# Background steps held behind a weight load, and gate products spread over two kinds of PSUM banks, in a two-layer decoder trunk

## The chip, the core and the metric

The kernel runs on one core of a Trainium2 chip. A core has TensorE for matmuls (PE in the profile, with its weight loads as PEld), VectorE (DVE), ScalarE (ACT), GpSimd (POOL) and SyncE (SP), which here issues nearly all DMAs. The metric is the time of one execution on the device in microseconds (us), the median of several runs; lower is better.

## What is computed

A trunk of two layers over one sequence of 1024 tokens with 1024 features, all in float32. Layer 0 mixes tokens by attention, layer 1 by a state-space scan with a gated output. Each mixer is followed by a channel mixer with 4096 hidden features. All four are wrapped in a modulation (scale, shift, gate) that comes from one vector c, and in a layer norm:

```
for i in range(2):
    shift, scale, gate = modulation(silu(c), mod_mix_w[i], mod_mix_b[i])
    h = x * (1 + scale) + shift
    y = mla_mixer(h, ...) if i == 0 else s5_mixer(h, ...)
    x = layer_norm(ALPHA * x + (1 + gate) * y, ...)
    shift, scale, gate = modulation(silu(c), mod_ffn_w[i], mod_ffn_b[i])
    h = x * (1 + scale) + shift
    a = relu(h @ w1[i] + b1[i]);  y = (a * a) @ w2[i] + b2[i]
    x = layer_norm(ALPHA * x + (1 + gate) * y, ...)

# the end of s5_mixer
g = gelu(y)
z = g * sigmoid(g @ w_glu + b_glu)
return z @ w_out
```

## The kernel before

**Products in three passes.** Every large product splits both float32 operands into a high part (rounded for TensorE's fast float32 format) and a low part, the rest, and sums three matmuls: high by high, high by low, low by high. `split` makes the two parts, the high one on ScalarE (L74) and the low one on VectorE or GpSimd (L75); `mm3` issues the three matmuls (L78, L79, L80). So one block of 128 hidden features against 512 tokens is 8 x 3 = 24 matmuls of 128 x 128 by 512.

**Stages in time.** Attention runs to about 444 us, with its output product; the first channel mixer from there to 1222; the state-space mixer to about 1440; its gate products to 1532; its output product to 1645; the second channel mixer to the end. The parameters of the state-space mixer and the modulations of layer 1 do not depend on x. They are computed in the background of the first channel mixer.

**PSUM in these stages.** There are eight banks of 128 x 512 float32: two for transposes (tag `tr`), two for first products (`psA`, tag `a1`, in the profile `a`, taken by `a1_tile`) and four for the wide products (`psM`, tag `mm`, taken by `mm_half`, or two at a time by `mm_tile`).

**The channel mixer** (`mlp`, a generator that its caller drives step by step). The hidden features come in NJ = 32 blocks. `load1(j)` loads a block of w1 (512 KB on SP, L997) and splits it; `load2(j)` loads a block of w2 (L1004), multiplies it by the gate row (L1005) and splits it. Both loads use the same two raw buffers (tag `wr`). `mm1(j, h)` computes one block of hidden features for one half of the tokens into an `a1` bank: 24 matmuls, relu and square on ScalarE (L1026, L1027), the high part (L1028) and the low part on VectorE (L1029), which frees the bank. `mm2(js, h)` multiplies two blocks by w2 for four tiles of 128 tokens, each into two `mm` banks, and `accumulate` adds them to the rows X on VectorE (L829).

The head of the mixer loads three blocks of w1, runs five first products while the last rows still come from attention, loads two blocks of w2, and has GpSimd turn all eight row tiles into the residual (`residual`, L885 and L886). The last rows are normed on VectorE (L849 to L860) and ScalarE, transposed on TensorE (L874), scaled on ScalarE (L877) and split (L880, L881) into `hT`. Then a loop over g from 0 to 13 does per round two loads of each kind, four first products (three in the round g = 0, since its first was done in the head) and the wide products of the two blocks before.

**The background.** `bg` chains 48 steps of the two modulations, one flush and 75 steps of `s5_params`. A step of a modulation (`mod_block`) loads two pieces of a modulation weight, 256 KB each, on SP (L561) into small raw buffers, and folds each into an accumulator: the first of eight on GpSimd (L563), the others on VectorE (L568). `hv` holds these buffers: two accumulators and two raw ones (named `mb` in the profile), and from the product of block 5 on four raw ones more (`mr`). At the end of eight pieces TensorE sums the accumulator over partitions by small matmuls (L582, L588). `mlp` calls `tick(w)` after each first product with w = 2 and after each tile of a wide product with w = 1; a credit grows by w times `pace`, and each whole credit runs one step of `bg`. What is left at the first tile of the last wide product is run at once (`finish0`).

**The gate products.** For each of eight blocks m of w_glu, the block is loaded (L1466) and split, then each half of the tokens gets a product of 24 matmuls into an `a1` bank, a sigmoid (L1475), a multiplication by g (L1476) and a split into `zT`. The output product (`o_tiles`) follows; its first call works on three tiles of tokens at once, two in four `mm` banks and the third in the two `a1` banks.

**What sets the order.** The Python program traces all instructions; a planner at compile time then orders each engine's instructions along a simulated timeline, the earlier traced first where several are ready, and a tile waits until a buffer of its tag is free. Each engine and each DMA queue then runs its list strictly in that order. `tc.issue_after(ins)` adds an order without a wait: what the block traces on the engine of `ins` is listed behind `ins`.

Of the kernel before, what the change touches and what calls it, by code (L numbers as in the profile page):

```python
# [39 lines left out]
def kernel(  # L40
# [13 lines left out]
    V, S, P, PE, SY = nc.vector, nc.scalar, nc.gpsimd, nc.tensor, nc.sync  # L54
# [18 lines left out]
    def split(hi, lo, src, eng=None):  # L73
        S.activation(hi, src, AF.Copy)  # L74
        (eng or V).tensor_tensor(lo, src, f32(hi), ALU.subtract)  # L75
# [221 lines left out]
    ps = tr4()  # L297
# [161 lines left out]
    for t in range(8):  # L459
        zn[t] = f0.tile([128, 512], F32, tag="zn", name="zn", bufs=8)  # L460
        if t == 7:
            for v, vt in ((v1, vt1), (v2, vt2)):
                ps = tr4()
# [58 lines left out]
    gffn = cst.tile([128, 1024], F32, name="gffn")  # L522
# [90 lines left out]
    def step(gen, n=1, late=0):  # L613
        if late:
            with tc.high_priority(offset=-late):
                step(gen, n)
            return
        for _ in range(n):
            next(gen, None)
# [3 lines left out]
    bg = chain(mod_block(mod_mix_w[0], mod_mix_b[0], None, 2, "row", grow, pj, hv, on_pool=True),  # L623
               mod_all(0, mod_ffn_w[0], mod_ffn_b[0], 48, 0, 0, gffn, pj, hv, on_pool=True), mod_flush(hv))
# [194 lines left out]
    def mm_half():  # L819
        return psM.tile([128, 512], F32, tag="mm", name="mm")  # L820
# [13 lines left out]
    def a1_tile():  # L834
        return psA.tile([128, 512], F32, tag="a1", name="a1")
# [85 lines left out]
    wp = pool("wp", bufs=2)  # L921
# [6 lines left out]
    rb = res_row(wp, ln_mix_b[0], gb2=(gffn, mlp_b2[0]))  # L928
# [24 lines left out]
    hT = [[pa2.tile([128, 8, 512], F32R, tag="pa", name="hT") for _ in range(2)], None]  # L953
# [24 lines left out]
    def mlp(l, hT, bufs_, gate, wp, bg, finish, w1x, rb, pace=0.0):  # L978
        w1b, w2b, ab = bufs_
        w1r = mlp_w1[l].rearrange("(k p) (j f) -> j p k f", p=128, f=128)  # L980
        last = NJ - 1

        def w1_buf(j):
            return w1x if j == 0 else w1b[j % 2]

        def w2_buf(j):
            return w2b[j % 3] if j < last else tuple(q.rearrange("p k f -> p (k f)") for q in w1b[1])

        def a2_buf(j, h):
            return ab[3 * h + j % 3] if j < last else w1b[0][h].rearrange("p k f -> p (k f)").rearrange(  # L990
                "p (s f) -> p s f", s=2)

        def load1(j):
            if j >= NJ:
                return
            r = wp.tile([128, 8, 128], F32, tag="wr", name="w1r")
            SY.dma_start(r, w1r[j])  # L997
            split(*w1_buf(j), r)

        def load2(j):  # L1000
            if j >= NJ:
                return
            r = wp.tile([128, 1024], F32, tag="wr", name="w2r")
            d = SY.dma_start(r, mlp_w2[l][j * 128:(j + 1) * 128, :])  # L1004
            V.tensor_tensor(r, r, gate, ALU.mult)  # L1005
            split(*w2_buf(j), r)
            return d.ins

        credit = [0.0]

        def tick(w):
            credit[0] += w * pace
            while credit[0] >= 1.0:
                step(bg)
                credit[0] -= 1.0

        def mm1(j, h):
            wh, wl = w1_buf(j)
            hh, hl = hT[h]
            ps = a1_tile()  # L1020
            for k in range(8):
                mm3(ps, wh[:, k], wl[:, k], hh[:, k], hl[:, k], k == 0, k == 7)
            if l == 0 and j == 5 and h == 0:
                hv.r += Halves([wp.tile([128, 1024], F32, tag="r4", name="mr", bufs=2) for _ in range(2)]).all
            a2 = a2_buf(j, h)
            S.activation(ps, ps, AF.Relu, bias=vt2[:, l * 32 + j:l * 32 + j + 1])  # L1026
            S.activation(ps, ps, AF.Square)  # L1027
            S.activation(a2[:, 0], ps, AF.Copy)  # L1028
            V.tensor_tensor(a2[:, 1], ps, f32(a2[:, 0]), ALU.subtract)  # L1029
            tick(2.0)  # L1030

        def mm2(js, h):
            for t in range(4 * h, 4 * h + 4):
                ps = mm_tile()
                sl = slice((t % 4) * 128, (t % 4) * 128 + 128)
                for hf in range(2):
                    cs_ = slice(hf * 512, hf * 512 + 512)
                    for j in js:
                        a2, (wh, wl) = a2_buf(j, h), w2_buf(j)
                        mm3(ps[hf], a2[:, 0, sl], a2[:, 1, sl], wh[:, cs_], wl[:, cs_], j == js[0], j == js[-1])  # L1040
                if js[-1] == last:
                    finish(t, ps)
                else:
                    accumulate(t, ps)
                    tick(1.0)

        for j in range(3):
            load1(j)
        split_ = yield
        for j in range(3):  # L1050
            mm1(j, 0)
            split_ = (yield) or split_
        mm1(0, 1)
        mm1(1, 1)
        with tc.issue_after(split_):
            load2(0)
            d = load2(1)
        with tc.issue_after(d):
            ra = res_row(wp, ln_mix_g[l], name="ra")
        for t in range(8):  # L1060
            residual(t, ra, rb)
        for g in range(NJ // 2 - 2):
            j = 2 * g + 2
            load1(j + 1)
            if g:
                mm1(j, 0)
            mm1(j, 1)
            load2(j)
            mm2((j - 2, j - 1), 0)
            load1(j + 2)  # L1070
            mm1(j + 1, 0)
            mm2((j - 2, j - 1), 1)
            mm1(j + 1, 1)
            load2(j + 1)
        load1(last)
        mm1(last - 1, 0)
        mm1(last - 1, 1)
        load2(last - 1)
        mm1(last, 0)
        mm1(last, 1)  # L1080
        load2(last)
        js = tuple(range(NJ - 4, NJ))
        mm2(js, 0)
        mm2(js, 1)
# [8 lines left out]
    for t in range(2, 8):  # L1093
        ps = o_tiles([nxt], WO.__getitem__, t == 7)[0]
# [264 lines left out]
        if t == 5:  # L1359
            u_load(0)  # L1360

    mixer = mlp(0, hT, cont, gffn, wp, bg, finish0, w1x, rb, pace=0.6)
    next(mixer)
    mixer.send(o_end(7, ps))
    step(mixer, 100)
# [98 lines left out]
    for m in range(8):  # L1464
        r = wp.tile([128, 8, 128], F32, tag="wr", name="wgr")
        SY.dma_start(r, wgr[m])  # L1466
        gh, gl = [wp.tile([128, 8, 128], F32R, tag=g, name="wg", bufs=n)
                  for g, n in ((("r4", 2), ("r4", 2)) if m % 2 == 0 else (("k4", 1), ("a4", 1)))]
        split(gh, gl, r)
        for hf in range(2):  # L1470
            sl = slice(hf * 512, hf * 512 + 512)
            ps = a1_tile()
            for k in range(8):
                mm3(ps, gh[:, k], gl[:, k], gTh[k][:, sl], gTl[k][:, sl], k == 0, k == 7)
            S.activation(ps, ps, AF.Sigmoid, bias=vt1[:, VGLU + m:VGLU + m + 1])  # L1475
            V.tensor_tensor(ps, gTf[m][:, sl], ps, ALU.mult)  # L1476
            split(zT[hf][0][:, m], zT[hf][1][:, m], ps)
# [95 lines left out]
```

## Time and profile before

| | us |
|---|---|
| timed runs, median of 3 | 2366.98 |
| lowest and highest of them | 2361.97, 2376.51 |
| the profiled execution | 2353.56 |
| its span, first to last instruction | 2351.4 |
| VectorE busy in the span | 1420.1 (60%) |
| ScalarE busy | 831.6 (35%) |
| GpSimd busy | 626.5 (27%) |

The mean granted clock of TensorE over the span is 0.978 of full speed. A row of the windows gives a stretch, its length, the busy time and number of instructions of PE, PEld, DVE, ACT and POOL, the granted clock, and the busy share and rate of the DMA engines. A row of the timeline gives start, duration, engine, line, operation and operands, and in brackets how long the engine had been idle and what ended that. A row of the waits gives who waited for whom: total us, times, longest. Matmuls overlap in the pipeline, so their durations add up to more than the time they take.

### The profile page before, as it was taken

To read this page: it belongs to the slowest core of one execution; us is meant where nothing else is said; L and a number is where in the kernel's file an instruction comes from. 1 tells how busy PE (TensorE), PEld (TensorE's weight loads), DVE (VectorE), ACT (ScalarE), POOL (GpSimd) and SP (SyncE) were. 2 spreads that over 40 slices of the span, in tenths; PEclk is the share of its full clock that TensorE was granted. 3 is DMA by queue.
4 is the path that set the end of the run, shared out by engine and by line. 5 is a ranking of instruction groups with operands and counts; after the bars stand their busy time and mean duration, and the time that the engine had idled before them with its cause. 6 is when DMAs were issued, how large, how long until landed. Compare 5 with 4: busy or idle time off the path is not lost.

```text
span 2351.4 us, 29181 instructions
## 1 busy us (share of the span) xinstructions
PE 2241.3 (95%) x11039; PEld 1885.4 (80%) x11039; DVE 1420.1 (60%) x2473; ACT 831.6 (35%) x1399; POOL 626.5 (27%) x731
## 2 busy tenths in 40 slices
PE   7799998979999999999998998999999999999996
PEld 6678886867788788888888997878788888888885
DVE  8877786387777766676444445454744444444437
ACT  3477774442222323333235233324322222222321
POOL 5534767371000334333021212433500000000005
PEclk8899998989999999999999999999999999999998
DMA  7222224135453345446123554330211111111201
GB/s 257 62 62 61 85 99 170 32 111 167 150 163 113 96 110 144 127 116 158 51 81 144 162 167 157 108 99 28 72 54 45 45 59 40 54 54 36 63 27 72
DMA packets 191579, 229.44 MB, mean 98 GB/s; under 512 B 45361, under 2 KB 136764, under 8 KB 189390
## 3 DMA queue, kind: packets, MB, share of 16 engines
q1 hardware_dynamic: 186558, 214.98, 29.4%
q0 software_dynamic: 3840, 12.59, 1.7%
q8 instruction: 87, 1.43, 0.2%
q14 instruction: 54, 0.44, 0.1%
q10 hardware_dynamic: 1040, 0.00, 0.0%
HBM read 190.88 MB, written 34.54 MB: 96 GB/s over the span
## 4 chain that ended last, share of the span: by engine, by line
PE 48%; DVE 3%; DMA 2%; ACT 1%; issue 1%; SPq 0%; POOL 0%; DVEq 0%; ACTq 0%; POOLq 0%
PE a L78 8%; PE a L80 8%; PE a L79 8%; PE mm L78 7%; PE mm L79 7%; PE mm L80 7%; PE mm L1392 1%; DMA wor<-in_ssm_w_out_dram 1%; DMA pt<-prm_d 1%; DVE ct L75 1%; PE a L1419 0%; PE a L1418 0%; PE a L1417 0%; DVE wo L75 0%; DVE X L1518 0%
## 5 line engine op out<-in xcount | busy, mean ns | idle before, releaser
L829 DVE TENSOR_TENSOR X<-X,mm 128x512 f32<-128x512 f32 x478 | 322.6, 684 | 286.1 <-PE mm L80 282.2
L78 PE MATMUL mm<-pb 128*128 128x512 f32 x512 | 203.0, 397 | 5.8 <-DVE X L829 5.8
L78 PE MATMUL a<-hT,pb 128*128 128x512 f32 x496 | 195.6, 394 | 11.0 <-DVE pb L1029 10.7
L79 PE MATMUL mm<-pb 128*128 128x512 f32 x512 | 199.7, 390 | 0.0
L80 PE MATMUL mm<-pb 128*128 128x512 f32 x512 | 199.7, 390 | 0.0
L80 PE MATMUL mm<-ct 128*128 128x512 f32 x512 | 199.2, 389 | 0.0
L79 PE MATMUL mm<-ct 128*128 128x512 f32 x512 | 199.2, 389 | 0.0
L78 PE MATMUL mm<-ct 128*128 128x512 f32 x512 | 198.5, 390 | 0.0
L78 PE MATMUL a<-hT,ct 128*128 128x512 f32 x496 | 193.3, 390 | 3.3 <-DVE ct L1029 3.3
L1026 ACT ACTIVATE a<-a,vt 128x512 f32<-128x512 f32 x128 | 83.5, 652 | 314.5 <-PE a L80 314.3
L80 PE MATMUL a<-hT,pb 128*128 128x512 f32 x496 | 194.4, 392 | 0.0
L79 PE MATMUL a<-hT,pb 128*128 128x512 f32 x496 | 194.4, 392 | 0.0
L80 PE MATMUL a<-hT,ct 128*128 128x512 f32 x496 | 193.1, 389 | 0.0
L79 PE MATMUL a<-hT,ct 128*128 128x512 f32 x496 | 193.0, 389 | 0.0
L885 POOL TENSOR_TENSOR X<-X,rb 128x1024 f32<-128x1024 f32 x6 | 14.8, 2480 | 634.5 <-ACT X L861 634.5
L1005 DVE TENSOR_TENSOR w2r<-w2r,gffn 128x1024 f32<-128x1024 f32 x64 | 87.6, 1371 | 132.4 <-DMA w2r<-in_mlp_w_dram 132.3
L78 PEld LDWEIGHTS a<-hT,pb 128*128 128x128 f32 x496 | 94.0, 190 | 31.7 <-DVE pb L1029 12.4
L78 PEld LDWEIGHTS mm<-pb 128*128 128x128 f32 x512 | 96.2, 188 | 27.3 <-DVE X L829 7.5
L78 PEld LDWEIGHTS mm<-ct 128*128 128x128 f32 x512 | 95.9, 188 | 20.9 <-DVE X L829 0.6
L80 PEld LDWEIGHTS mm<-pb 128*128 128x128 f32 x512 | 96.1, 188 | 20.2
L79 PEld LDWEIGHTS mm<-ct 128*128 128x128 f32 x512 | 96.2, 188 | 20.0
L79 PEld LDWEIGHTS mm<-pb 128*128 128x128 f32 x512 | 96.2, 188 | 19.7 <-issue 0.7
(492 smaller groups left out, 5414.5 us busy)
## 6 DMA issues: line engine op xcount, KB each, us to landing
w1r<-in_mlp_w_dram SPq DMA_DIRECT2D x64, 512.0 KB, 4.1
w2r<-in_mlp_w_dram SPq DMA_DIRECT2D x64, 512.0 KB, 3.3
pt<-prm_d SPq DMA_DIRECT2D x16, 1536.0 KB, 7.2
mb<-in_mod_mix_w_dram SPq DMA_DIRECT2D x41, 256.0 KB, 2.6
prm_d<-cb SPq DMA_DIRECT2D x80, 128.0 KB, 2.4
wm<-in_mod_mix_w_dram SPq DMA_DIRECT2D x8, 1024.0 KB, 11.8
mb<-in_mod_ffn_w_dram POOLq DMA_DIRECT2D x32, 256.0 KB, 3.0
mb<-in_mod_ffn_w_dram SPq DMA_DIRECT2D x32, 256.0 KB, 3.0
```

What stands on the lines that cost most here:

```text
L75: (eng or V).tensor_tensor(lo, src, f32(hi), ALU.subtract)
L78: PE.matmul(ps, lh, rh, start=start, stop=False)
L79: PE.matmul(ps, lh, rl, start=False, stop=False)
L80: PE.matmul(ps, ll, rh, start=False, stop=stop)
L829: V.tensor_tensor(xh, xh, ps[h], ALU.add)
L885: P.tensor_tensor(X[t], X[t], ra, ALU.mult)
L1005: V.tensor_tensor(r, r, gate, ALU.mult)
L1026: S.activation(ps, ps, AF.Relu, bias=vt2[:, l * 32 + j:l * 32 + j + 1])
L1392: PE.matmul(pvv[i][:, g * 128:g * 128 + 128], pt[:, i, g], ug[:, g], start=True, stop=True)
```

## The change

In `mlp`, `load1` now returns the DMA of the block it loads. `tick` does nothing, and counts no credit, until the list `behind` has an entry. In the loop each round with g > 0 appends the DMA of its `load1(j + 1)`; the first is that of block 5, the sixth load of w1, in the round g = 1. From then on each background step is traced inside `issue_after` of that DMA, so that the DMAs it issues on SP stand behind it in SP's list. The pace goes from 0.6 to 0.66 for the first channel mixer; the second has an empty background. In the gate products the second half of the tokens takes its bank from the four `mm` banks instead of the two `a1` banks.

```diff
@@ load1 @@
-            SY.dma_start(r, w1r[j])
+            d = SY.dma_start(r, w1r[j])
             split(*w1_buf(j), r)
+            return d.ins
@@ tick @@
         credit = [0.0]
+        behind = []
 
         def tick(w):
+            if not behind:
+                return
             credit[0] += w * pace
             while credit[0] >= 1.0:
-                step(bg)
+                with tc.issue_after(behind[0]):
+                    step(bg)
                 credit[0] -= 1.0
@@ the loop of mlp @@
             j = 2 * g + 2
-            load1(j + 1)
+            d = load1(j + 1)
             if g:
+                behind.append(d)
                 mm1(j, 0)
@@ the first channel mixer @@
-    mixer = mlp(0, hT, cont, gffn, wp, bg, finish0, w1x, rb, pace=0.6)
+    mixer = mlp(0, hT, cont, gffn, wp, bg, finish0, w1x, rb, pace=0.66)
@@ the gate products @@
-            ps = a1_tile()
+            ps = a1_tile() if hf == 0 else mm_half()
```

## The prediction

> **What bounds the kernel now.** I read the page's first part, then the windows by stage, then TensorE's waits stage by stage, and at last the timelines of the two places where TensorE waits.
>
> ```profile
> PE 2241.3 (95%) x11039; PEld 1885.4 (80%) x11039; DVE 1420.1 (60%) x2473; ACT 831.6 (35%) x1399; POOL 626.5 (27%) x731
> ```
> ```profile
> 480.00:560.00 80.00, 63.83 (x268) 51.78 (x267) 67.70 (x69) 25.45 (x42) 50.91 (x20) 0.87 0.41 133
> 560.00:600.00 40.00, 38.15 (x172) 31.32 (x171) 26.91 (x38) 11.18 (x16) 0.69 (x1) 1.00 0.52 159
> 600.00:1222.00 622.00, 619.72 (x2841) 512.15 (x2840) 410.18 (x752) 181.40 (x293) 141.29 (x153) 1.00 0.42 118
> 1440.00:1532.00 92.00, 88.40 (x392) 72.46 (x391) 37.80 (x42) 31.34 (x44) 38.82 (x31) 1.00 0.30 98
> ```
>
> The columns are the stretch, its length, the busy time of PE, PEld, DVE, ACT and POOL, the granted clock and the DMA share. TensorE sets the time: it is busy 95% of the span, and in the long loop of the first channel mixer (600 to 1222 us) it is idle for 2.3 us in 622. What can be won lies where it is idle. Two such places are touched: the head of the first mixer, idle 80 - 63.83 + 40 - 38.15 = 18.0 us, and the gate products, idle 3.6 us. Who ends these waits, in the head and then in the gate products:
>
> ```profile
> PE a L78 <- DVE pb L1029: 10.7, 1, 10.7
> PE mm L78 <- DVE X L829: 4.9, 3, 1.9
> PE tr L588 <- DVE mb L568: 2.2, 1, 2.2
> ```
> ```profile
> PE a L78 <- DVE zT L75: 3.4, 1, 3.4
> ```
>
> In the head every wait is for VectorE, which is busy 67.7 of the 80 us. What fills it (VectorE's groups, 476 to 536 us):
>
> ```profile
> L568 DVE SCALAR_TENSOR_TENSOR mb<-mb,csT 128x512 f32<-128x512 f32 x12 | 24.5, 2041 | 1.3 <-DMA mb<-in_mod_mix_w_dram 0.7 <-POOL mb L563 0.5
> ```
>
> L568 is a background step. Twelve of them take 24.5 us of 60, at 2041 ns each. In the loop, with GpSimd's residual rows done, the same operation is short:
>
> ```profile
> L568 DVE SCALAR_TENSOR_TENSOR mb<-mb,csT 128x512 f32<-128x512 f32 x17 | 12.8, 750 | 0.5
> ```
>
> After two of the waits the clock drops:
>
> ```profile
> 495.00:500.00 5.00, 4.91 (x14) 3.68 (x15) 3.58 (x8) 3.66 (x8) 5.00 (x3) 0.50 0.19 56
> 500.00:505.00 5.00, 5.00 (x20) 4.04 (x19) 5.00 (x2) 1.06 (x1) 5.00 (x3) 0.84 0.00 0
> 525.00:530.00 5.00, 3.33 (x8) 2.66 (x9) 5.00 (x4) 0.00 (x0) 5.00 (x2) 0.50 0.53 160
> 530.00:535.00 5.00, 5.00 (x19) 3.98 (x18) 5.00 (x4) 0.14 (x1) 4.36 (x2) 0.77 0.59 207
> ```
>
> Busy time times the missing part of the clock gives 4.91 x 0.50 + 5.00 x 0.16 = 3.3 us and 3.33 x 0.50 + 5.00 x 0.23 = 2.8 us lost. So the head can yield at most 10.7 + 4.9 + 2.2 + 3.3 + 2.8 = 23.9 us, and the gate products 3.4 us.
>
> **The change part by part.** Before, a tick comes 24 units ahead of group g = 1 (five first products of 2, then the group g = 0 with three more products and eight tiles), which makes 24 x 0.6 = 14 background steps. The mixer has 240 units. After, the first 24 do nothing and the other 216 run at 0.66: 142 steps in place of 144. The background has 124 (48 for the two modulations, 1 flush, 75 for the state-space parameters), so it ends at unit 24 + 124/0.66 = 212 in place of 207, still 28 units, nearly two groups, ahead of the end. Nothing is removed; 14 steps go from the head into the 13 groups behind, with 28 loads on SP, 24 or 25 operations of L568 (the first of every eight is GpSimd's) and their small matmuls.
>
> **Term 1, the long wait.** VectorE before the product that TensorE waits for:
>
> ```profile
> 511.02 2.87 DVE L568 SCALAR_TENSOR_TENSOR mb<-mb,csT 128x512 f32<-128x512 f32 x1 [0.52 <-POOL mb L563]
> ...
> 517.17 2.81 DVE L568 SCALAR_TENSOR_TENSOR mb<-mb,csT 128x512 f32<-128x512 f32 x1
> ...
> 520.02 2.71 DVE L568 SCALAR_TENSOR_TENSOR mb<-mb,csT 128x512 f32<-128x512 f32 x1
> 522.66 3.35 DVE L75 TENSOR_TENSOR pb<-w2r,pb 128x1024 fp32r<-128x1024 f32 x1
> 525.94 0.68 DVE L1029 TENSOR_TENSOR pb<-a,pb 128x512 fp32r<-128x512 f32 x1
> ```
>
> Only two `a` banks exist, and L1029 at 525.94 frees one. Ahead of it on VectorE stand three background operations, 2.87 + 2.81 + 2.71 = 8.4 us; without them it comes 8.4 us earlier and 2.3 us of the wait stay. If what stands further ahead moves up too (term 2), nothing stays. So 8.4 to 10.7 us; I take the middle, 9.5. A rest of 2.3 us or less is shorter than the 3.4 us wait in the gate products, which no lower clock follows (the window from 1440 has 1.00), so the 2.8 us of clock come back too: **12.3 us**, bounds 8.4 and 13.5. What is late next is the w2 split itself (3.35 us at 522.66), which has no background in it and stays.
>
> **Term 2, the first wait.**
>
> ```profile
> 485.27 1.08 DVE L568 SCALAR_TENSOR_TENSOR mb<-mb,csT 128x512 f32<-128x512 f32 x1 [0.70 <-DMA mb<-in_mod_mix_w_dram]
> ...
> 486.40 2.75 DVE L568 SCALAR_TENSOR_TENSOR mb<-mb,csT 128x512 f32<-128x512 f32 x1
> 489.08 0.20 DVE L860 TENSOR_SCALAR bnm<-bmv,bny 128x1 f32<-128x1 f32 x1
> ```
> ```profile
> 491.20 1.47 PE L874 MATMUL mm<-ident,X 128*128 128x128 f32 x12
> 494.87 1.84 PE L588 MATMUL tr<-ones,mb 128*128 128x1 f32 x8 [2.20 <-DVE mb L568]
> 496.79 0.80 PE L78 MATMUL a<-hT,w1x 128*128 128x512 f32 x1
> ```
> ```profile
> 496.08 0.66 ACT L880 ACTIVATE hT<-mm 128x512 fp32r<-128x512 f32 x1
> ```
>
> The last row's normalisation is stretched by background steps (1.08 + 2.75 us and 0.70 us of waiting for their load, 4.5 us), but the transposes behind it stand in TensorE's order where the compile-time schedule put them, at 491.20 behind two products. If they stay there, hT still lands at 496.74 and the gap from 492.67 to 496.79 is as long as now: gain 0. If the schedule, which also loses these steps, puts them some 4 us ahead, the 2.2 us and the 3.3 us of clock are won, 5.5 us. I take the middle, **2.7 us**, since no row tells the new order. The Trainium skill (TensorE: Matmul & The Clock Gate, HAM oscillation — how this bites in real kernels) has the rule that no gap of TensorE should pass about 3.4 us, else the clock is halved. The trace agrees so far: the 10.7 us wait is followed by a clock of 0.50, the 3.4 us wait by none. It speaks against half of this term: with the transposes unmoved the gap of 4.1 us halves the clock again, and the term is 0; with them moved it is 5.5.
>
> **Term 3, the X waits, 4.9 us.** They come at 550 to 595 us, where VectorE, in order, sits behind background steps that wait for their own loads:
>
> ```profile
> DVE mb L568 <- DMA mb<-in_mod_mix_w_dram: 12.1, 12, 3.3
> ```
>
> That is 12 waits with 3.3 us as the longest, because only two raw buffers are free until the product of block 5 adds four more. After the change 8 units x 0.66 = 5 steps run with two buffers, before it 32 x 0.6 = 19. The stall is partly gone and partly moved to g = 1: bounds 0 and 4.9, taken **2.0**.
>
> **Term 4, the moved steps.** 25 x 750 ns = 19 us of VectorE go into 13 groups. The cover is VectorE's idle time, 622 - 410 = 212 us there. The fullest stretch with background, and one near the end without it:
>
> ```profile
> 760.00:780.00 20.00, 20.00 (x90) 16.57 (x89) 18.36 (x67) 3.31 (x5) 3.92 (x6) 1.00 0.27 73
> ...
> 1120.00:1140.00 20.00, 20.00 (x90) 16.57 (x89) 10.21 (x12) 6.64 (x9) 0.00 (x0) 1.00 0.24 80
> ```
>
> The mixer alone takes about 10.2 of 20, the background 18.4 - 10.2 = 8.2; at 0.66/0.6 = 1.1 times that it is 9.0, in all 19.2 of 20. It fits, barely. TensorE's idle time in the loop is now 2.3 us; I take **1.5 us more**, an estimate, bounds 0 and 24.7 (the third rival).
>
> **The new place in SP's queue.** Background loads now stand behind the load of block 5:
>
> ```profile
> 540.93 0.38 SPq L997 DMA_DIRECT2D w1r<-in_mlp_w_dram  x1
> ```
>
> Its wait for a buffer holds up only the background behind it, and no weight load then stands behind a background load in the head. I cost the order itself at nothing; if it delayed the background's end, two groups of slack cover it.
>
> **Term 5, the gate products.**
>
> ```profile
> 1455.55 0.50 PE L78 MATMUL a<-gT,wg 128*128 128x512 f32 x1 [3.38 <-DVE zT L75]
> ```
> ```profile
> 1443.38 1.59 DVE L75 TENSOR_TENSOR wg<-wgr,wg 128x1024 fp32r<-128x1024 f32 x1 [2.63 <-ACT wg L74]
> ```
>
> The second block's weights are split by 1444.97; its first product waits only for an `a` bank, until 1455.55. With half the products in the four `mm` banks the second `a` bank is free, and TensorE goes on: **3.4 us**. What follows (the output weights wait for gT, the reload for gTf) hangs on the end of the last product and moves with it. Against it: the output product then finds one of its four `mm` banks still in evacuation, in place of one `a` bank; the last evacuation shows how long:
>
> ```profile
> 1532.26 0.66 ACT L1475 ACTIVATE a<-a,vt 128x512 f32<-128x512 f32 x1 [0.71 <-PE a L80]
> ```
> ```profile
> 1534.90 0.69 DVE L75 TENSOR_TENSOR zT<-a,zT 128x512 fp32r<-128x512 f32 x1 [0.67 <-ACT zT L74]
> ```
>
> From 1532.26 to 1535.59 are 3.3 us; nine matmuls of the three other `mm` banks cover 9 x 88.4/392 = 2.0 us of it, so up to 1.3 us would be lost. Bounds 2.1 and 3.4.
>
> **Sum.** 12.3 + 2.7 + 2.0 - 1.5 + 3.4 = 18.9 us. The profiled execution took 2353.56 us (span 2351.4, 2.2 around it), so it would take 2334.7. The three timed runs had a median of 2366.98 (2361.97 to 2376.51), 13.4 above the profiled one; I give the time against that median: 2366.98 - 18.9 = **2348**, 0.8% less.
>
> **The rivals.**
> *Everything comes back.* Transposes ahead, no X waits, no price in the loop: 23.9 + 3.4 = 27.3 us, 2340. For it: VectorE loses 24.5 of 60 us in the head. Against: L568 waits for loads wherever it starts.
> *The stall moves.* Background starts at g = 1 with a burst, and the X waits and part of the long wait come again there: term 1 at its low end 8.4, terms 2 and 3 at 0, 4.9 us of new waits: 8.4 + 3.4 - 4.9 = 6.9 us, 2360. Against: at g = 1 GpSimd's residual is done, and L568 takes 750 ns and not 2041.
> *Slower: VectorE fills up in the loop.* If the denser background keeps each X evacuation back once a group by the longest such wait seen, 1.9 us, the 13 groups cost 24.7 us against 20.4 of the other terms: 2371. It decides from the point where mixer and background pass 20 of 20, a background of 9.8 where I have 9.0, a pace of 0.72. Against: at 18.36 of 20 TensorE is not idle at all.
> *The change does not do what it says:* the schedule already interleaves the halves of a gate product, and term 5 could be 0; it is inside the range.
>
> **How the numbers follow.** Forecast (gain 10 to 23 us) 0.57; everything back 0.20; the stall moves 0.17; slower 0.06. One per cent, about what a measurement of this kernel can tell from no change, is 23.7 us, so faster by over 1% needs nearly all of the first rival: 0.22 with the scatter of the runs. Slower by over 1% needs more than the last rival: 0.04. Within: 0.74. The range goes from the first rival less half the runs' spread, 2333, to just above the second with the same, 2366.
>
> **What would show it.** Right: no L568 and no L588 before about 530 us, TensorE's 10.7 us wait under 3 us, the clock at 1.00 from 525 to 535, no wait at the second gate block, the mixer's loop with under 5 us of waits. Term 2 is decided by where the twelve transposes stand behind the products. Wrong: waits for X of over 10 us in the loop, or VectorE at 20 of 20 there, or a new wait of the output product for an `mm` bank.

## The result, and the profile after

The changed kernel takes 2335.48 us, the median of 4 runs (2334.04 to 2338.89), where the kernel before takes 2365.04 beside it (4 runs, 2361.97 to 2376.51): a ratio of 0.9868, 95% interval 0.9833 to 0.9904. Two repeats with more runs gave 2340.52 beside 2359.28 (0.9929, 0.9902 to 0.9957) and 2340.28 beside 2357.88 (0.9922, 0.9902 to 0.9941). So the change gains 17.6 to 18.8 us in the repeats and 29.6 in the first comparison; the repeats are the better measured. The profiled execution took 2335.68 us (span 2333.8), 17.9 under that of before.

The page's first line, and the windows of the same four stretches. The gate products come about 20 us earlier now; their window is moved by 18.

```profile
PE 2231.1 (96%) x11039; PEld 1876.9 (80%) x11039; DVE 1406.1 (60%) x2473; ACT 832.2 (36%) x1399; POOL 632.9 (27%) x731
```
```profile
480.00:560.00 80.00, 71.77 (x308) 56.76 (x307) 56.60 (x59) 28.68 (x45) 48.89 (x19) 0.98 0.37 116
560.00:600.00 40.00, 40.00 (x182) 33.25 (x181) 23.92 (x33) 9.74 (x14) 0.69 (x1) 1.00 0.31 98
600.00:1222.00 622.00, 617.05 (x2841) 511.16 (x2840) 416.52 (x778) 186.16 (x302) 154.17 (x174) 1.00 0.45 127
1422.00:1514.00 92.00, 91.78 (x418) 76.23 (x419) 41.28 (x45) 33.07 (x47) 42.05 (x32) 1.00 0.31 100
```

In the head TensorE is idle for 8.23 + 0 us where it was 16.17 + 1.85, and the clock is 0.98 where it was 0.87. VectorE does 11 us less there. In the loop TensorE's idle time grows from 2.28 to 4.95 us; in the gate products it falls from 3.6 to 0.2. Who ends the waits now, in the head (476 to 600 us), in the loop, and from the gate products through the output product:

```profile
PE mm L78 <- DVE X L829: 4.0, 2, 3.5
PE a L78 <- DVE pb L1034: 3.3, 2, 1.7
PE mm L78 <- ACT pb L74: 0.7, 1, 0.7
```
```profile
PE a L78 <- DVE pb L1034: 2.3, 1, 2.3
PE mm L78 <- DVE X L829: 1.4, 1, 1.4
...
```
```profile
PE mm L78 <- DVE X L829: 1.6, 1, 1.6
PE mm L79 <- DVE wo L75: 1.5, 1, 1.5
```

The 10.7 us wait for the pb split is gone, as are the wait of the small matmuls (2.2) and that for zT (3.4). New in the head is one X wait of 3.5 us. Of the two waits in the output product, the one for X stands in the trace of before as well (1.7 us); the one for the split of the output weights (1.5 us) does not, but a second trace of the same kernel (e1, below) has it with 0.8. SP's queue at the same place:

```profile
473.74 2.07 SPq L1005 DMA_DIRECT2D w2r<-in_mlp_w_dram  x2
...
526.59 0.38 SPq L997 DMA_DIRECT2D w1r<-in_mlp_w_dram  x1
527.07 0.52 SPq L561 DMA_DIRECT2D mb<-in_mod_mix_w_dram  x1
```

The first background load (L561) follows right behind the sixth load of w1. What VectorE does from 476 to 536 us in place of the twelve background operations of 2041 ns:

```profile
L1006 DVE TENSOR_TENSOR w2r<-w2r,gffn 128x1024 f32<-128x1024 f32 x4 | 9.7, 2450 | 5.9 <-DMA w2r<-in_mlp_w_dram 5.9
L75 DVE TENSOR_TENSOR pb<-w2r,pb 128x1024 fp32r<-128x1024 f32 x3 | 9.0, 2997 | 0.0
...
L568 DVE SCALAR_TENSOR_TENSOR mb<-mb,csT 128x512 f32<-128x512 f32 x2 | 1.5, 751 | 3.7 <-DMA mb<-in_mod_mix_w_dram 3.7
```

L568 is down to two operations at their short price. VectorE now waits for the loads of w2 (5.9 us), and its gatings still take twice what one takes alone (1.21 us where GpSimd is done, below), with GpSimd's residual beside them.

**Where the time came from.** Two stretches carry most of it, and both repeat well from trace to trace, where the start of the first mixer alone scatters (473.2 to 477.8 us in five traces without the change of the head). The first mixer, from its first product with w1x to the first store of a row of X to x_d; the rows of these two in the kernel before and in the changed one:

```profile
L78 PE MATMUL a<-hT,w1x x32: 389/389/795, 473.5 to 1653.8; 128*128 128x512 f32 x32
L1356 SPq DMA_DIRECT2D x_d<-X x8: 319/320/339, 1217.1 to 1246.2; - x8
```
```profile
L78 PE MATMUL a<-hT,w1x x32: 389/389/496, 470.2 to 1634.3; 128*128 128x512 f32 x32
L1362 SPq DMA_DIRECT2D x_d<-X x8: 319/320/339, 1203.6 to 1232.6; - x8
```

That is 1217.1 - 473.5 = 743.6 before and 1203.6 - 470.2 = 733.4 after. The other, from the last load of the state-space parameters to the last gate product, is 109.2 before and 104.1 after. The table gives both for every trace; the difference between kernels is read here and not from single times. What the two stretches do not carry lies ahead of the first mixer for a part: between the first traces of before and after, its start alone makes 473.5 - 470.2 = 3.3 us of the 17.6 between the spans, and no part of the change is shown to cause it.

| kernel | median (runs) | before beside it | ratio, 95% interval | first mixer | gate stretch |
|---|---|---|---|---|---|
| before, profiled | | | | 743.6 | 109.2 |
| after | 2335.48 (4) | 2365.04 | 0.9868, 0.9833 to 0.9904 | 733.4 | 104.1 |
| e5, after again | 2340.52 (6) | 2359.28 | 0.9929, 0.9902 to 0.9957 | 732.5 | 105.9 |
| e12, after again | 2340.28 (6) | 2357.88 | 0.9922, 0.9902 to 0.9941 | 733.3 | 104.1 |
| e1, before again | 2360.10 (12) | 2362.64 | 0.9989, 0.9964 to 1.0014 | 745.9 | 109.8 |
| e2, head alone | 2346.42 (6) | 2362.64 | 0.9924, 0.9897 to 0.9951 | 733.2 | 111.5 |
| e3, gates alone | 2361.29 (12) | 2362.64 | 0.9989, 0.9962 to 1.0016 | 745.3 | 105.2 |
| e9, gates alone | 2356.41 (12) | 2359.63 | 0.9986, 0.9972 to 1.0001 | 743.8 | 105.1 |
| e4, no order on SP | 2351.95 (8) | 2362.64 | 0.9943, 0.9921 to 0.9966 | 741.3 | 104.1 |
| e11, order alone, credits kept | 2357.76 (12) | 2357.88 | 0.9993, 0.9979 to 1.0007 | 749.9 | 104.8 |
| e8, order behind block 3 | 2344.74 (6) | 2359.28 | 0.9933, 0.9919 to 0.9947 | 737.1 | 104.7 |
| e6, pace 0.6 | 2343.32 (7) | 2359.28 | 0.9932, 0.9908 to 0.9956 | 734.2 | 105.1 |
| e7, residual behind the gating | 2338.54 (6) | 2359.28 | 0.9908, 0.9892 to 0.9923 | 728.2 | 105.1 |
| e10, gates alone, same residual | 2353.23 (11) | 2359.63 | 0.9970, 0.9958 to 0.9981 | 744.8 | 105.1 |

### The profile page after: what moved, and what is told of

The parts are those of the page before. It is cut to its first block, busy times and chain, and to the rows that moved or that the text cites. A ratio compares the mean times of both kernels' runs of the same rounds, so it can differ in the third digit from the quotient of the medians.

```text
span 2333.8 us, 29199 instructions
## 1 busy us (share of the span) xinstructions
PE 2231.1 (96%) x11039; PEld 1876.9 (80%) x11039; DVE 1406.1 (60%) x2473; ACT 832.2 (36%) x1399; POOL 632.9 (27%) x731
## 4 chain that ended last, share of the span: by engine, by line
PE 78%; DVE 11%; DMA 4%; ACT 3%; issue 2%; POOL 1%; SPq 1%; DVEq 0%; ACTq 0%; POOLq 0%
PE mm L79 11%; PE mm L80 11%; PE mm L78 11%; PE a L78 11%; PE a L79 11%; PE a L80 11%; DMA w2r<-in_mlp_w_dram 1%; PE mm L1398 1%; DVE pb L75 1%; DVE macc L337 1%; DVE w2r L1006 1%; PE tr L752 1%; DMA wor<-in_ssm_w_out_dram 1%; DVE X L829 1%; DMA mb<-in_mod_ffn_w_dram 1%
## 5 line engine op out<-in xcount | busy, mean ns | idle before, releaser
L79 PE MATMUL mm<-pb 128*128 128x512 f32 x512 | 200.3, 391 | 0.0
L78 PEld LDWEIGHTS mm<-pb 128*128 128x128 f32 x512 | 96.3, 188 | 28.5 <-DVE X L829 7.4
L78 PEld LDWEIGHTS mm<-ct 128*128 128x128 f32 x512 | 95.9, 188 | 22.4 <-ACT ct L74 2.3
L80 PEld LDWEIGHTS mm<-pb 128*128 128x128 f32 x512 | 96.3, 188 | 20.3
L79 PEld LDWEIGHTS mm<-ct 128*128 128x128 f32 x512 | 96.2, 188 | 20.0
L80 PEld LDWEIGHTS mm<-ct 128*128 128x128 f32 x512 | 96.2, 188 | 19.9
```

The lines of the kernel that those rows point to most:

```text
L78: PE.matmul(ps, lh, rh, start=start, stop=False)
L79: PE.matmul(ps, lh, rl, start=False, stop=False)
L80: PE.matmul(ps, ll, rh, start=False, stop=stop)
```

## The experiments

**The two parts apart (e1, e2, e3, e9).** e1 is the kernel before, unchanged. e2 takes the gate part out of the changed kernel, e3 is the kernel before with that part alone, and e9 is e3 a second time:

```diff
-            ps = a1_tile() if hf == 0 else mm_half()
+            ps = a1_tile()
```

> The kernel before once more, unchanged, for a second trace of it and for its scatter. The question: the two traces put 17.6 us between the spans of before and after, the medians 29.6 us; which of the two is the change? Theory A (the traced run of before was a lucky one): the spread of before is its own, a new trace shows a span of about 2360 us, with more or longer waits or more slow clock than the 2351.4 us trace. Theory B (the medians are the accident): a new trace shows about 2351 us again, and the ratio to the kernel before, 1.000, has an interval of under 0.3% either way.

> Only the first mixer's part of the change (deferred background, order on SP, pace 0.66); the gate products keep both halves in the a banks. Theory A (the two parts add, the head gives about 10 us by the traces and the gate products 3.4): 3.4 us slower than the changed kernel, with the 3.4 us wait back in the second gate block; about 2339 us. Theory B (the gain of the gate products is given back in the output product, where the changed kernel shows new waits of 1.5 us for a wo tile and of 1.6 us for X): no slower than the changed kernel by more than 1.5 us.

> Only the gate products' part: second halves in the mm banks; the background as before. Theory A: the wait of 3.4 us at the second block goes and nothing else changes before that stage, 3.4 us less than the kernel before, 0.9986 of it. Theory B (given back in the output product): within 1.5 us of the kernel before, with the end of the output product no earlier against the end of the scan than before.

> The kernel before with the second half of each gate product in the wide products' banks alone, a second time, beside the next kernel. Theory, that some executions lose some 13 to 18 us at the head of the second channel mixer, where GpSimd's residual rows lock out one operation of VectorE: again two clumps of runs, one at 2353 to 2359 and one at 2364 to 2372, and in a traced run of the upper one an operation of VectorE of over 10 us between 1640 and 1690 us. Rival, that the upper clump was that chip's scatter at that hour: one clump, within 8 us, like the runs of the kernel before.

The stretches fall apart cleanly. The four traces with the whole head part (after, e5, e12, e2) have a first mixer of 732.5 to 733.4, the four with the head of before (before, e1, e3, e9) one of 743.6 to 745.9: 11.5 us between the means (733.1 and 744.65). With the gate part its stretch lies between 104.1 and 105.9, without it between 109.2 and 111.5. The output product behind it (from the last gate product to the last product with the output weights) takes 92.8 to 93.9 us in the three traces without the gate part and 92.6 to 95.1 in the eleven with it, 0.8 more in the mean. From the last load of the parameters to the end of that product it is 202.0 to 205.3 us without and 197.9 to 200.3 with the gate part, 4.5 between the means. So the gain is not given back, as the second theories of e2 and e3 had it.

e1 gives the yardstick of the times: the same kernel against itself, 0.9989, and its span of 2354.4 us is nearer to the 2351 of its second theory than to the 2360 of the first. In the times the gate part does not show: it is worth 1.4 and 3.2 us, each time with an interval that reaches 1, and e2, without it, has the same ratio as the changed kernel (0.9924 beside 0.9929 and 0.9922). The head alone is worth 16 us in the medians, more than its stretch; the scatter of the runs does not allow more. One of the six runs of e5 lies at 2359.48, 22.8 us above the lowest, and has no trace; none of e12 lies above 2344.70.

e3 also showed something that no theory had. Five of its twelve runs took 2366.20 to 2371.40 us. The profiled one is among them, with 2369.29, and the loss is at the head of the second mixer, which nothing in the edit touches. VectorE, GpSimd and TensorE's wait there:

```profile
1651.75 20.78 DVE L1005 TENSOR_TENSOR w2r<-w2r,gffn 128x1024 f32<-128x1024 f32 x1
...
1672.45 1.21 DVE L1005 TENSOR_TENSOR w2r<-w2r,gffn 128x1024 f32<-128x1024 f32 x1
```
```profile
1648.26 11.71 POOL L886 TENSOR_TENSOR X<-X,rb 128x1024 f32<-128x1024 f32 x5
...
1664.49 6.96 POOL L886 TENSOR_TENSOR X<-X,rb 128x1024 f32<-128x1024 f32 x3
```
```profile
PE mm L78 <- ACT ct L74: 18.2, 1, 18.2
```

One gating is recorded with 20.78 us, the next, with GpSimd done, with 1.21. It ends at 1672.53, 1.08 us, about its own length, after GpSimd's last row (1664.49 + 6.96 = 1671.45); meanwhile GpSimd runs its rows at their short price, 2.34 us each. At the same place the kernel before shares:

```profile
1650.94 5.88 DVE L1005 TENSOR_TENSOR w2r<-w2r,gffn 128x1024 f32<-128x1024 f32 x2
```
```profile
1647.68 14.73 POOL L886 TENSOR_TENSOR X<-X,rb 128x1024 f32<-128x1024 f32 x5
```

Here each of the two pays, VectorE 2.94 us for an operation, GpSimd 2.95 for a row, and none is shut out. e9 did not settle how often the other thing happens: ten of its runs lie from 2350.48 to 2360.58 and two at 2365.05 and 2365.72, and its trace shows the two engines sharing. So the gates' small gain can be hidden by it, as in e3, but that all of the spread between runs comes from there is not shown.

**The order taken out (e4).**

```diff
-                with tc.issue_after(behind[0]):
-                    step(bg)
+                step(bg)
```

> The changed kernel without the order behind the sixth load of w1: background deferred to the round g = 1 by the empty credit alone, pace 0.66. Theory A (what pays is that the 14 steps leave the head, the order on SP costs and gives nothing): the planner may list some background loads a little earlier, the same time as the changed kernel within 3 us. Theory B (the order is what keeps the loads out of the head, since the planner lists ready loads early): background loads and L568 operations before 525 us again, TensorE's waits in the head up by 5 us or more.

The credits still begin at the same place, but the head is nearly that of before. SP's queue, VectorE's group (482 to 542 us, as the first mixer starts late here, at 479.2) and TensorE's waits in the head of e4:

```profile
472.81 6.66 SPq L561 DMA_DIRECT2D mb<-in_mod_mix_w_dram  x3
482.67 0.33 SPq L1005 DMA_DIRECT2D w2r<-in_mlp_w_dram  x1
483.33 0.33 SPq L561 DMA_DIRECT2D mb<-in_mod_mix_w_dram  x1
```
```profile
L568 DVE SCALAR_TENSOR_TENSOR mb<-mb,csT 128x512 f32<-128x512 f32 x10 | 17.9, 1790 | 1.5 <-DMA mb<-in_mod_mix_w_dram 0.9 <-POOL mb L563 0.5
```
```profile
PE a L78 <- DVE pb L1033: 5.4, 2, 5.2
PE mm L78 <- DVE X L829: 4.4, 1, 4.4
PE tr L588 <- DVE mb L568: 2.4, 1, 2.4
```

The first background load goes out at 472.81, before the loads of w2, although its step is traced in the round g = 1. The planner lists an instruction where its engine and its buffers are free, and the background has nothing else to wait for. So the credits say where a step is traced, not where it runs; only the order keeps it out of the head. Without the order the first mixer takes 741.3 us, a gain of 3 where the whole part has 11.5, and the median is 5.5 us above that of e2 beside it, though e4 has the gate part. The second theory held in kind; of its 5 us of waits 4 came (TensorE idle for 12.3 us in the first 85 of the mixer in place of 8.2), and a lower clock came with them (0.88 in place of 0.98).

**The order alone (e11), with e12 as the changed kernel beside it.**

```diff
+            credit[0] += w * pace
             if not behind:
                 return
-            credit[0] += w * pace
```

> The changed kernel, but the 24 units ahead of the sixth load of w1 keep counting: the credits pile up and 24 x 0.66 = 15 steps are traced at once at the first tick behind that load. So the order on SP stands alone, without the deferral by credit. Theory, that the order does nearly all of it: within 2 us of the changed kernel, the stretch from the first w1 product to the first store of layer 0's gated state 732 to 736 us. Rival, that the stall then moves to the round g = 1 (the second rival of the prediction): 4 to 8 us slower than the changed kernel, with waits for X or the pb split of over 4 us in sum between 535 and 600 us. Rival, that the credits matter as much as the order: as slow as the kernel without the order, 8 us or more.

> The changed kernel once more, beside it: median 2335 to 2341, ratio 0.987 to 0.993. If the long runs of it are the same rare event as before, at most 2 of 6 to 12 runs lie over 2350.

My theory that the order does nearly all of it fell. With the credits kept, 26 x 0.66 = 17 steps are traced at the first tick behind the sixth load (15 of them from the head), and all of the head's gain is lost again: 749.9 us for the first mixer, 16.6 more than e12, and a ratio of 0.9993. The second rival came: the first mixer is 8.6 us longer even than without the order (741.3). TensorE's idle time in the head is as short as in the changed kernel (7.4 us in 480 to 560); most of the loss comes behind it. TensorE's stretches, its waits from 535 to 700 us and VectorE's waits there, all of e11:

```profile
560.00:600.00 40.00, 34.31 (x160) 27.52 (x158) 26.02 (x39) 7.42 (x11) 1.38 (x2) 1.00 0.60 179
600.00:700.00 100.00, 96.15 (x418) 77.66 (x418) 77.22 (x115) 22.54 (x32) 6.92 (x7) 0.97 0.66 200
```
```profile
PE mm L78 <- DVE X L829: 5.1, 6, 2.1
...
PE a L78 <- DVE pb L1034: 1.5, 1, 1.5
...
```
```profile
DVE mb L568 <- DMA mb<-in_mod_mix_w_dram: 23.9, 23, 2.8
```

In the two windows TensorE is idle for 5.69 and 3.85 us, where e12 has 0.80 and 0, and from 600 to 620 us its clock is 0.84. And the row of e12 for VectorE's waits:

```profile
DVE mb L568 <- DMA mb<-in_mod_mix_w_dram: 8.4, 6, 3.0
```

Steps that are traced before the product of block 5 know only the two raw buffers; with the credits kept these are (24 + 8) x 0.66 = 21 steps, in the changed kernel 8 x 0.66 = 5. From 535 to 700 us VectorE runs 50 operations on those two buffers in e11 and 25 in e12, and waits 23 times for a load in place of 6. These waits stand in VectorE's list ahead of evacuations of X and of splits. It is the second rival of the prediction, and dearer than that had it: it left a gain of 6.9 us, and here nothing is left. Whether the two buffers make the price, or the number of steps that are let go at once, is not shown: no run gives such a burst more buffers.

**The place of the order (e8) and the pace (e6).** e8 puts the first entry of the list at the load of block 3, one round earlier; e6 sets the pace back.

```diff
             d = load1(j + 1)
+            behind.append(d)
             if g:
-                behind.append(d)
                 mm1(j, 0)
```

> The changed kernel with the list filled one round earlier: the first entry is the load of block 3 (round g = 0) in place of that of block 5, and ticks count from there. Theory, that what pays is that the background's loads on SP no longer stand ahead of the head's weight loads: the first background load goes out behind that of block 3, still behind both w2 loads of the head, so the long wait for the pb split stays away, but the steps run with two raw buffers beside the residual of GpSimd and the X waits at 550 to 595 us come back: 2 to 6 us slower than the changed kernel. Rival, that any order on SP does it: within 1.5 us. Rival, that only a start after the residual helps: as slow as the changed kernel without the order, 8 us or more above it.

> The changed kernel with a pace of 0.6 in place of 0.66. My theory, that the place behind the sixth load of w1 pays and the pace does nothing: within 2 us of the changed kernel, with 0 to 1 us less idle time of TensorE in the loop from 600 to 1222 us. Rival, that a denser background costs what term 4 took (1.5 us) or more: 2 to 5 us faster. Rival, that at 0.6 the background runs late (unit 24 + 124/0.6 = 231 of 240): the rest is run at the last wide product and it is 2 us or more slower.

e8 has a first mixer of 737.1, 4 us more than the changed kernel, and its median is 4.2 over e5: the theory's 2 to 6, though the intervals of the two times overlap. From 535 to 600 us the waits for X that it wanted back are 1.2 us, beside 2.3 for the pb split; the changed kernel has neither. The wait for the pb split stays small (2.3 us at the longest), and VectorE waits for background loads 15 times, which in the changed kernel it does 6 times in the same stretch (476 to 600 us; e8, then after):

```profile
DVE mb L568 <- DMA mb<-in_mod_mix_w_dram: 14.8, 15, 2.3
```
```profile
DVE mb L568 <- DMA mb<-in_mod_mix_w_dram: 7.6, 6, 2.5
```

The pace changes nothing that could be measured: 734.2 us of first mixer and a ratio of 0.9932 beside 0.9929. The median is 2.8 us above that of e5, with intervals that overlap, so the rival with a late background is not excluded by the times. TensorE's idle time from 600 to 1222 us is 5.6 us, where the theory wanted less than the 4.95 of the changed kernel.

**GpSimd's residual behind the gating (e7, e10).** The scaling of the gain row `ra`, for which all residual rows wait, goes to VectorE behind the gating of the second w2 block; e7 does it to the changed kernel, e10 to the gates alone.

```diff
@@ res_row @@
-        if al != 1.0:
+        if behind is not None:
+            with tc.issue_after(behind):
+                V.tensor_scalar(r, r, al, 0.0, ALU.mult, ALU.add)
+        elif al != 1.0:
@@ mlp @@
-            ra = res_row(wp, ln_mix_g[l], name="ra")
+            ra = res_row(wp, ln_mix_g[l], name="ra", behind=g_)
```

> The changed kernel with one edit: the scaling of the residual's gain row, on which all of GpSimd's residual rows wait, goes from GpSimd to VectorE and is listed there behind the gating of the second block of w2. So GpSimd's residual starts only when VectorE has both gatings behind it, in both channel mixers. Theory, that GpSimd's residual rows stretch VectorE's operations at the mixers' heads, and in some runs lock it out for 20 us: the two gatings take 1.1 to 1.3 us each in place of 2.1 to 2.9, no run lies more than 6 us above the lowest, and the median is 2 to 6 us below the changed kernel. Rival, that the same contention only moves to the splits and accumulations behind: median within 2 us of the changed kernel. Rival, that the residual rows come late and TensorE waits for the first X rows: 3 to 10 us slower, with waits for X in the loop's first round over 5 us.

> The same with the scaling of the residual's gain row on VectorE behind the gating of the second w2 block, so that GpSimd's residual starts only behind both gatings. Theory of the lock-out: no upper clump, all runs within 8 us, lowest at 2348 to 2354, median 4 to 10 us under that of the kernel with the gates alone. Rival, that the lock-out finds another operation (the splits behind the gatings run beside the residual now): the upper clump stays, with another line's operation of over 10 us in a traced run of it. Rival, that the upper clump has nothing to do with these two engines: it stays, with no long operation of VectorE in a traced run of it.

VectorE's groups of e7 from 476 to 536 us:

```profile
L75 DVE TENSOR_TENSOR pb<-w2r,pb 128x1024 fp32r<-128x1024 f32 x3 | 9.8, 3282 | 0.0
...
L1009 DVE TENSOR_TENSOR w2r<-w2r,gffn 128x1024 f32<-128x1024 f32 x4 | 6.8, 1716 | 5.7 <-DMA w2r<-in_mlp_w_dram 5.7
```

The gatings fall from 2450 to 1716 ns, the splits of w2 behind them pay more (2997 to 3282), and the first mixer is 5 us shorter in the trace (728.2). So the theory held in part: it wanted 1.1 to 1.3 us for a gating, and the contention also moved on, as its rival said. In the times the 5 us do not show: 2338.54 beside 2340.52, with intervals that overlap, and with 8.8 us between the shortest and the longest run where the theory wanted 6. e10 is 3.2 us under e9, and no upper group shows among its runs (2346.03 to 2357.12). But the lock-out theory wanted 4 to 10 us, all runs within 8 us (they spread over 11.1) and a lowest of 2348 at least, and e9 had only two long runs of twelve, so e10 proves little; its first mixer, 744.8, is no shorter than without the edit. The version of e7 is no slower than the changed kernel, and whether it is faster stays open.

## Why the prediction was right, and where not

**The sum** was 18.9 us. Against the profiled execution it said 2334.7, and the three executions of the changed kernel that were profiled took 2335.68, 2336.67 and 2337.17. The medians of the repeats differ by 18.8 and 17.6. The size and the sign were right, but that they fit so closely is in part luck: the stretches account for 11.5 + 4.5 = 16.0 us, the start of the mixer gave 3.3 us to the pair of traces that no term had, and the terms missed to both sides and nearly cancelled.

**The base** put the time too high: 2366.98, a median of three runs 13.4 over the profiled one, was carried over whole. In later sets of 12 to 25 runs the median of the same kernel was 2357.88 to 2362.64. The middle between that median and the profiled run, 2360.3, lies within 2.4 us of all of them. Against the repeats (2340.4) the forecast is 7.7 us high, and its base is 8.4 above the two medians measured beside them. The 12.5 us against the first four runs are another matter: there the base fits the kernel before within 2 us, and the four runs of the changed kernel are short.

**Term 1 (12.3 us): right for its wait, wrong for what follows.** The rest of the long wait is 1.68 us, inside the 2.3 that the prediction left, and the clock stays at 1.00 behind it. But the clock came back only in part, through a wait that was not foreseen. TensorE's rows, and the clock there, of the changed kernel:

```profile
518.27 0.50 PE L78 MATMUL a<-hT,pb 128*128 128x512 f32 x1 [1.68 <-DVE pb L1034]
523.89 0.50 PE L78 MATMUL mm<-pb 128*128 128x512 f32 x1 [3.52 <-DVE X L829]
```
```profile
520.00:525.00 5.00, 1.48 (x7) 0.92 (x6) 3.90 (x3) 1.24 (x3) 5.00 (x2) 1.00 0.07 29
525.00:530.00 5.00, 4.57 (x15) 3.15 (x14) 5.00 (x7) 0.00 (x0) 3.79 (x2) 0.66 0.44 126
```

What is late next is not the w2 split, as the prediction had it, but the accumulation into X: on VectorE it stands behind a gating that waits 2.89 us for its w2 load. The clock falls to 0.66 for 5 us, 4.57 x 0.34 = 1.6 us. Of the 13.5 us of wait and clock before, the two pb waits (3.3), the X wait (3.5) and its clock (1.6) leave 5.1.

The Trainium skill (TensorE: Matmul & The Clock Gate, HAM oscillation — how this bites in real kernels) has the rule that no gap of TensorE should pass about 3.4 us. Two waits agree with it, 3.52 us followed by 0.66 here and 3.38 us followed by 1.00 in the gate products of before. The other traces speak against a sharp limit. In e1, the same kernel as before, the same wait of 3.38 us is followed by 0.66, and in the trace of before itself a wait of 1.76 us at 1426.39, among the small products of the scan, is too (e1, then before):

```profile
1455.00:1460.00 5.00, 4.40 (x13) 3.55 (x14) 1.24 (x2) 0.60 (x1) 0.10 (x1) 0.66 0.68 213
```
```profile
1425.00:1430.00 5.00, 3.61 (x18) 3.62 (x19) 4.01 (x10) 0.00 (x0) 2.37 (x2) 0.66 0.88 322
```

So the prediction's ground for the 2.8 us of clock, that a wait shorter than 3.4 us costs none, came true in the head, but the traces do not bear it as a rule.

**Term 2 (2.7 us, between 0 and 5.5): the upper end came.** The transposes moved up: they stand 485.48 - 470.2 = 15.3 us behind the first product with w1x, in place of 491.20 - 473.5 = 17.7, and the rest of a product behind them covers the way to hT:

```profile
485.48 1.47 PE L874 MATMUL mm<-ident,X 128*128 128x128 f32 x12
...
490.12 0.50 PE L79 MATMUL a<-hT,w1x 128*128 128x512 f32 x1 [0.23 <-DVE hT L881]
```

A wait of 0.23 us and no lower clock (1.00 from 485 to 505 us) is left there; the 2.2 and the 3.3 us were won.

**Term 3 (2.0 us): too small.** No X wait is left from 535 to 600 us. e11 fits the prediction's mechanism: 5 steps on the two raw buffers left no X wait there, 21 let go in a burst cost all of the head's gain.

**Term 4 (1.5 us): too small as well, and by another way.** The loop's idle time grew by 2.7 us, and 1.1 us of clock were lost there. VectorE's fullest 20 us hold 19.49 of 20 (800 to 820 us), where the prediction had 19.2, and TensorE is not idle in them. The longest wait, 2.32 us, stands at 1122.35, behind a gating that waits for its load; VectorE and SP there:

```profile
1120.47 1.23 DVE L1006 TENSOR_TENSOR w2r<-w2r,gffn 128x1024 f32<-128x1024 f32 x1 [6.69 <-DMA w2r<-in_mlp_w_dram]
```
```profile
1115.44 0.38 SPq L1005 DMA_DIRECT2D w2r<-in_mlp_w_dram  x1
```

SP issues this load in the middle of 16 loads for the scan (L1385, 1111.56 to 1120.89), which go out once the parameters are done, and the DMA engines are busy all the time from 1115 to 1125. The clock behind the wait is 0.73. In the kernel before these 16 loads go out in one piece and no load of w2 falls among them. e6, with the old pace, has the same wait (2.12 us at 1173.41), so the pace is not the reason; whether it is the later end of the background was not tested.

Together the head won 18.0 - 8.2 = 9.8 us of idle time and 5.7 - 1.5 = 4.2 us of clock (summed over windows of 5 us), and the loop gave back 2.7 and 1.1: 10.2 us, which is the difference between the stretches of these two traces, 743.6 - 733.4. The prediction had 15.5 for these four terms. Terms 2 and 3 came out 5.7 us over what was taken; the new X wait with its clock (3.5 + 1.6), the pb waits that stayed (3.3 + 0.7, where 1.2 had been left), two small waits (0.7) and the loop (2.3 more) took back 10.9.

**The order was costed at nothing, and that was the step that failed.** The prediction moved the 14 steps by counting credits in the order of the program. It noted that no weight load then stands behind a background load in the head, but gave that no price. e4 and e11 show that neither half does the work alone: credits without the order gain 3 us, the order without the credits loses 5, and both together gain 11.5. The order takes the steps out of the head, and the credits see to it that they do not come back as a burst on two raw buffers. The sum of the prediction could come out because the change has both.

**Term 5 (3.4 us, bounds 2.1 and 3.4): right.** The wait of 3.38 us is gone, and the gate stretch is 5.1 us shorter. TensorE's idle time and clock from the last load of the parameters to the end of the last gate product, before and after:

```profile
1422.20:1531.80 109.60, 103.34 (x503) 86.67 (x502) 50.59 (x69) 36.14 (x51) 45.00 (x37) 0.98 0.34 112
```
```profile
1407.50:1512.00 104.50, 101.61 (x511) 85.89 (x510) 51.48 (x70) 36.16 (x51) 47.57 (x37) 1.00 0.36 117
```

The idle time falls from 6.26 to 2.89 us, 3.4 as predicted; it is 2.6 to 2.9 us in all eleven traces with the gate part and 6.3 to 6.5 in the three without. The rest is clock, and between these two traces it is not the gate part's: it is the 0.66 from 1425 to 1430 us, ahead of the first gate product, and e5 and seven other traces with the gate part have such a dip too. In e1 and e2 the 3.38 us wait itself is followed by a lower clock, so that the gate part can also win some of it, which the prediction left out. The gate products also start earlier, with the half that has an `mm` bank (at 1419.3), while the state-space products ahead of them use the `a` banks until 1424. The output product gives back 0.8 us in the mean, within the 1.3 of the lower bound, but no new wait for an `mm` bank is seen: its X wait of 1.6 us was there before (1.7), and the one for the split of its weights is 0 to 2.1 us from trace to trace with the gate part, 0 to 0.8 without.

**The rivals.** That everything comes back, 27.3 us, did not happen; the first comparison reads like it (29.6), the repeats do not. The stall that moves is what e11 shows, and it needs the credits kept. VectorE came close to filling up in the loop, with 19.49 of 20, but TensorE did not wait there. Of the signs of being right one failed, the clock at 1.00 from 525 to 535 us.

## What to carry to other kernels

Where a planner lists instructions by when their engines and buffers are free, placing background work later in the program does not make it run later; it needs an order on the queue that feeds it, and a limit on how much is released at once. Count what a released burst does to the smallest buffer that feeds it, when its engine has urgent work as well: here a burst on two raw buffers stood between a gain of 11.5 us and a loss of 5. When a prediction is worked out on one profiled execution, give the time against that execution and treat the median of a few runs as one more sample.

## What the runs showed of the hardware

VectorE and GpSimd, each with two operands in SBUF, mostly share: both at about 2.9 us where alone they take 1.2 and 2.34. But in one trace VectorE's operation waited through the rest of GpSimd's run of rows and took 20.78 us, and TensorE, which waited 18.2 us for what followed, went on at a mean clock of 0.59 from 1660 to 1680 us:

```profile
1660.00:1680.00 20.00, 6.33 (x22) 5.16 (x23) 17.22 (x6) 3.84 (x5) 11.45 (x5) 0.59 0.14 39
```

The Trainium skill (SBUF — State Buffer, 🔬 SBUF: two separate sides) describes the port pair of these two engines as an exclusive lock, which the one that starts first holds for its whole instruction. The usual case does not agree: one after the other, a gating and a row would take 1.21 + 2.34 = 3.55 us (an estimate from the two durations alone), and the trace of before shows both done in 2.95. The 20.78 us agree with a lock, but not with one that is handed over after an instruction; what decides between sharing and shutting out was not found, and only one of fourteen traces shows it.
